# Clearing the semaphores straight behind the waiting drain, without the plain drain in between

## The chip, the cores and the metric

The kernel runs on one core of one Trainium2 chip. The metric is the device time of one execution in microseconds; the medians of several runs are compared. Besides the time there is the **span**, from the first to the last of the program's own instructions, which the profile of one run shows. Most numbers below with three decimals are the nanosecond stamps of the trace, read from the span's start; the views of the profile round them to one decimal, and narrow stretches of a view bracket them. A run counts as slow if it lies over 1.5% above the fastest of its kernel.

Three words recur. A **semaphore** is a counter by which transfers and engines signal that they are done. A **barrier** is a place where every engine reports and waits until all have. A **drain** is an instruction for an engine's sequencer, the part that reads its instructions; what it waits for is told in the prediction.

I call **closing** the time from the end of GpSimd's last wait for stores to the end of the span. It is what the change works on.

## The reference

Two arrays of 32 x 256 x 1024 floats are interleaved element by element:

```
result = zeros((batch, seq, dim * 2), float32)
result[..., 0::2] = x
result[..., 1::2] = y
```

No arithmetic is done. 67.11 MB are read and 67.12 MB written, among them 8 KB of zeros that the kernel stores first and overwrites.

## The kernel before

Inputs are loaded in tiles of 128 partitions x 8192 floats by SyncE's queue, VectorE copies x to the even and y to the odd columns of an output tile, and ScalarE's queue stores each tile of 128 x 8192 floats:

```python
    for lw in lwidths:
        # (cut: tiles and access patterns)
        nc.sync.dma_start(out=xtile, in_=xs)
        nc.sync.dma_start(out=ytile, in_=ys)
        # (cut: two halves of the width, each:)
            nc.vector.tensor_copy(out=otile[:, 0::2], in_=xsub)
            nc.vector.tensor_copy(out=otile[:, 1::2], in_=ysub)
            nc.scalar.dma_start(out=os_, in_=otile)
```

When the program is built, the framework adds a closing block. In it SyncE would wait for all transfers, an all-engine barrier would follow, and GpSimd would clear the semaphores. The kernel already edits that block: the wait is handed to GpSimd, and the first barrier is cut out.

```python
    last = nc.main_func.blocks[-1]
    tail = last.instructions
    waits = [i for i in tail
             if i.engine == mybir.EngineType.SP
             and not i.sync_info.on_update and i.sync_info.on_wait]
    clear = next(n for n, i in enumerate(tail) if i.opcode == "ISA")
    # (cut: assertions)
    last.instructions = [
        copy.replace(i, engine=mybir.EngineType.Pool) for i in waits
    ] + tail[clear - 1 :]
```

As built, GpSimd's part of the block is: four pure waits for transfer semaphores (two each), a drain that waits for VectorE's semaphore, a **plain drain** (`tail[clear - 1]`), the clear of semaphores 99 to 107, and then GpSimd's share of a barrier over all five engines, which has a drain of its own. The builder marks the plain drain as one that comes ahead of the reset of a range of semaphores; the other two lack the mark.

Of the kernel before, what the change touches and what calls it, by code (L numbers as in the profile page):

```python
# [3 lines left out]

# [4 lines left out]


@with_exitstack
def _interleave(
    ctx: ExitStack,
    tc: tile.TileContext,
    x: bass.AP,
    y: bass.AP,
    out: bass.AP,
):
    nc = tc.nc  # L20
    P = 128

    total = 1
    for s in x.shape:
        total *= s

    WL = 8192
    WS = 4096

    xf = x.rearrange("b s d -> (b s d)")  # L30
    yf = y.rearrange("b s d -> (b s d)")
    of = out.rearrange("b s d -> (b s d)")

    fp32 = mybir.dt.float32

    xpool = ctx.enter_context(tc.tile_pool(name="xp", bufs=2))
    ypool = ctx.enter_context(tc.tile_pool(name="yp", bufs=2))
    opool = ctx.enter_context(tc.tile_pool(name="op", bufs=2))

    lwidths = [WL] * (total // P // WL)  # L40
    assert sum(lwidths) == total // P


    wpool = ctx.enter_context(tc.tile_pool(name="wp", bufs=1))
    zero = wpool.tile([16, 128], fp32, name="zero")
    nc.vector.memset(zero, 0.0)  # L46
    first = dataclasses.replace(of, offset=0, ap=[[2 * WL, 16], [1, 128]])
    nc.scalar.dma_start(out=first, in_=zero)

    start = 0  # L50
    for lw in lwidths:
        xtile = xpool.tile([P, WL], fp32, name="xtile")[:, :lw]
        ytile = ypool.tile([P, WL], fp32, name="ytile")[:, :lw]

        xs = dataclasses.replace(xf, offset=start, ap=[[lw, P], [1, lw]])
        ys = dataclasses.replace(yf, offset=start, ap=[[lw, P], [1, lw]])
        nc.sync.dma_start(out=xtile, in_=xs)
        nc.sync.dma_start(out=ytile, in_=ys)

        soff = 0  # L60
        while soff < lw:
            width = min(WS, lw - soff)
            otile = opool.tile([P, 2 * WS], fp32, name="otile")[:, : 2 * width]
            os_ = dataclasses.replace(
                of,
                offset=2 * start + 2 * soff,
                ap=[[2 * lw, P], [1, 2 * width]],
            )
            xsub = xtile[:, soff : soff + width]
            ysub = ytile[:, soff : soff + width]  # L70
# [3 lines that stand above are left out]
            soff += width  # L74

        start += P * lw
    assert start == total


def kernel(tc, x, y, out):  # L80
    nc = tc.nc
    _interleave(tc, x, y, out)
    tc.close()
    tc.compile()  # L84


    blocks = nc.main_func.blocks
    opening = blocks[0].instructions
    at, moved = next(
        (b, i)  # L90
        for b in blocks[1:]
        for i in b.instructions
        if i.engine == mybir.EngineType.SP and i.opcode == "DMACopy"
    )
    assert not moved.sync_info.on_wait
    body = at.instructions
    body.remove(moved)
    gate = next(
        n
        for n, i in enumerate(opening)  # L100
        if i.engine == mybir.EngineType.SP and i.opcode == "Drain"
    )
    opening.insert(gate, moved)
    at.instructions = body
    blocks[0].instructions = opening




    last = nc.main_func.blocks[-1]  # L110
    tail = last.instructions
    waits = [
        i
        for i in tail
        if i.engine == mybir.EngineType.SP
        and not i.sync_info.on_update
        and i.sync_info.on_wait
    ]
    clear = next(n for n, i in enumerate(tail) if i.opcode == "ISA")
    assert tail[clear].engine == mybir.EngineType.Pool  # L120
    assert tail[: len(waits)] == waits
    last.instructions = [
        copy.replace(i, engine=mybir.EngineType.Pool) for i in waits
    ] + tail[clear - 1 :]


# [1 line left out]
_INS = ['x', 'y']  # L128
_OUTS = [((32, 256, 2048), 'float32')]


# [23 lines left out]
```

## Time and profile before

| | before |
|---|---|
| time, median of the first 3 runs | 316.22 us (315.30 to 316.36) |
| span of the profiled run | 314.7 us |
| end of the last wait for stores | 314.108 us |
| closing | 0.594 us |

The profile's lines on the transfers, the closing and the three GpSimd drains stand in the prediction, with the way to read them.

### The profile page before, as it was taken

Reading aid. Unit: us, or ns where it says so; the run is one execution under the profiler, and the core shown is the slowest. Engines: PE = TensorE matmul, PEld = TensorE weight load, DVE = VectorE, ACT = ScalarE, POOL = GpSimd, SP = SyncE. Lnnn points to the kernel's source line nnn. Section 1 sums busy time; section 2 is a strip of 40 time slices with the busy share of each in tenths; the row PEclk is TensorE's granted clock in tenths of the full one; section 3 lists DMA queues with packets and bytes.
Section 4 is the critical chain, followed back from the end, with each engine's and each line's share of the span. In section 5 each row is a group of like instructions: output and inputs, shape, how many; then the busy total and the mean of one; then the engine's idle time right before and its main releaser. Section 6 shows DMA issues by size and latency. Waiting matters only on the chain.

```text
span 314.7 us, 141 instructions
## 1 busy us (share of the span) xinstructions
DVE 72.8 (23%) x33; POOL 0.2 (0%) x4
## 2 busy tenths in 40 slices
DVE  0433002223022320223103241041500405014500
POOL 0000000000000000000000000000000000000000
DMA  9999999999999999999999999999999999999996
GB/s 355 441 425 379 450 416 450 416 450 412 454 412 454 412 462 404 462 404 462 404 462 404 462 404 458 408 458 408 458 408 458 408 458 408 458 408 458 408 458 279
DMA packets 4640, 134.23 MB, mean 427 GB/s; under 512 B 528, under 2 KB 544, under 8 KB 544
## 3 DMA queue, kind: packets, MB, share of 16 engines
q1 hardware_dynamic: 2304, 67.11, 49.9%
q10 hardware_dynamic: 2336, 67.12, 49.4%
HBM read 67.11 MB, written 67.12 MB: 427 GB/s over the span
## 4 chain that ended last, share of the span: by engine, by line
DMA 83%; DVE 11%; DVEq 1%; issue 0%
DMA out_dram<-otile 76%; DMA ytile<-in_y_dram 7%; DVE otile L72 6%; DVE otile L71 5%; DVEq L84 1%; DVEq L71 0%
## 5 line engine op out<-in xcount | busy, mean ns | idle before, releaser
L71 DVE COPY otile<-xtile 128x4096 f32<-128x4096 f32 x16 | 36.6, 2295 | 190.5 <-DMA out_dram<-otile 179.0
L72 DVE COPY otile<-ytile 128x4096 f32<-128x4096 f32 x16 | 36.6, 2292 | 35.2 <-DMA ytile<-in_y_dram 35.2
L46 DVE MEMSET zero<- 16x128 f32 x1 | 0.2, 165 | 0.9 <-PEq L139 0.9
L139 POOL MEMSET const-bfloat16-1.0<- 128x1 bf16 x1 | 0.1, 101 | 0.0
L139 POOL MEMSET const-uint8-127<- 128x1 uint8 x1 | 0.1, 101 | 0.0
L139 POOL MEMSET const-float32-0.0<- 128x1 f32 x1 | 0.1, 98 | 0.2 <-issue 0.2
L139 POOL MEMSET const-float32-1.0<- 128x1 f32 x1 | 0.1, 98 | 0.0
## 6 DMA issues: line engine op xcount, KB each, us to landing
out_dram<-otile ACTq DMA_DIRECT2D x16, 4096.0 KB, 29.7
xtile<-in_x_dram SPq DMA_DIRECT2D x8, 4096.0 KB, 43.1
ytile<-in_y_dram SPq DMA_DIRECT2D x8, 4096.0 KB, 60.2
out_dram<-zero ACTq DMA_DIRECT2D x1, 8.0 KB, 6.6
```

What stands on the lines that cost most here:

```text
L46: nc.vector.memset(zero, 0.0)
L71: nc.vector.tensor_copy(out=otile[:, 0::2], in_=xsub)
L72: nc.vector.tensor_copy(out=otile[:, 1::2], in_=ysub)
L84: tc.compile()
L139: nc = _bacc.Bacc("TRN2", target_bir_lowering=False, num_devices=1)
```

## The change

The plain drain is left out, so that the clear comes straight behind the waiting drain:

```diff
-    waits = [
-        i
-        for i in tail
-        if i.engine == mybir.EngineType.SP
-        and not i.sync_info.on_update
-        and i.sync_info.on_wait
-    ]
+    wait = tail[0]
     clear = next(n for n, i in enumerate(tail) if i.opcode == "ISA")
 ... (assertions cut)
     last.instructions = [
-        copy.replace(i, engine=mybir.EngineType.Pool) for i in waits
-    ] + tail[clear - 1 :]
+        copy.replace(wait, engine=mybir.EngineType.Pool)
+    ] + tail[clear:]
```

Its intent is to shorten the path behind the last store by one instruction that has nothing to wait for.

More of the change, by code (lines that the diff above doesn't have):

```diff
@@ L111 @@
     tail = last.instructions
-    waits = [
-        i
-        for i in tail
-        if i.engine == mybir.EngineType.SP
-        and not i.sync_info.on_update
-        and i.sync_info.on_wait
-    ]
+    wait = tail[0]
     clear = next(n for n, i in enumerate(tail) if i.opcode == "ISA")
+    assert wait.engine == mybir.EngineType.SP and wait.opcode == "Drain"
+    assert wait.sync_info.on_wait and not wait.sync_info.on_update
     assert tail[clear].engine == mybir.EngineType.Pool
-    assert tail[: len(waits)] == waits
     last.instructions = [
-        copy.replace(i, engine=mybir.EngineType.Pool) for i in waits
-    ] + tail[clear - 1 :]
+        copy.replace(wait, engine=mybir.EngineType.Pool)
+    ] + tail[clear:]
 _INS = ['x', 'y']
```

## The prediction

> **What bounds the kernel now.** I read the page first, then the source-line view of the line that the closing instructions carry, then that view again in stretches of some 10 to 100 ns, to see the order of the last half microsecond. Of the page, these lines carry it:
>
> ```profile
> span 314.7 us, 141 instructions
> DVE 72.8 (23%) x33; POOL 0.2 (0%) x4
> DMA  9999999999999999999999999999999999999996
> HBM read 67.11 MB, written 67.12 MB: 427 GB/s over the span
> DMA 83%; DVE 11%; DVEq 1%; issue 0%
> ```
>
> The third line gives the busy share of the 16 DMA engines, in tenths, for 40 slices: 39 slices are nearly full and only the last one falls off. 134.23 MB pass in 314.7 us. VectorE, which does all the arithmetic, is busy for 23%, and its copies lie beside transfers. So the time is one long transfer, framed by an opening of under 1 us and a closing of about 2 us. The chain line of the page is to be read with care: it follows the last engine work back, and the last engine work is a VectorE copy that ends near 299.3 us. What comes later, the last store and the closing, isn't in it at all. For that I take the windows view, whose columns are the stretch, its length, VectorE and GpSimd busy time, TensorE clock, DMA share and GB/s:
>
> ```profile
> 306.00:312.00 6.00, 0.00 (x0) 0.00 (x0) 1.00 1.01 437
> 312.00:313.75 1.75, 0.00 (x0) 0.00 (x0) 1.00 0.05 19
> 313.75:314.11 0.36, 0.00 (x0) 0.00 (x0) 1.00 0.00 0
> 314.11:314.70 0.59, 0.00 (x0) 0.00 (x0) 1.00 0.00 0
> ```
>
> The transfer runs at full rate up to about 312, then few packets are left. In the last two rows none starts. This is where the change lies. The source-line view of the closing names each kind of sequencer instruction there, with count, shortest, median and longest duration in ns, and the start of the first and last one in us:
>
> ```profile
> L84 POOLq EVENT_SEMAPHORE  x6: 17/43/9673, 282.0 to 314.6; - x6
> L84 POOLq DRAIN  x3: 34/41/70, 314.2 to 314.4; - x3
> L84 PEldq DRAIN  x1: 8/8/8, 0.9 to 0.9; - x1
> L84 SPq DRAIN  x1: 130/130/130, 228.9 to 228.9; - x1
> L84 DVEq DRAIN  x1: 4475/4475/4475, 294.9 to 294.9; - x1
> L84 ACTq DRAIN  x1: 152/152/152, 299.7 to 299.7; - x1
> L84 POOLq EVENT_SEMAPHORE_RANGE_CLEAR  x1: 92/92/92, 314.3 to 314.3; - x1
> ```
>
> The 9,673 ns instruction is the wait for the last two stores. It ends just before 314.11: the stretch from 314.11 to 314.15 holds nothing on this line. The drains of the other four engines began at 0.9, 228.9, 294.9 and 299.7 us, so all four have long reached the closing barrier and wait there for GpSimd. After 314.11 GpSimd's sequencer is thus the only one with anything to do, and whatever it does lies on the path that sets the end, one instruction after the other.
>
> Three narrow stretches of the same view separate the three GpSimd drains. From 314.15 to 314.20, from 314.21 to 314.30 and from 314.43 to 314.50 they show, in that order:
>
> ```profile
> L84 POOLq DRAIN  x1: 41/41/41, 314.2 to 314.2; - x1
> ...
> L84 POOLq DRAIN  x1: 70/70/70, 314.2 to 314.2; - x1
> ...
> L84 POOLq DRAIN  x1: 34/34/34, 314.4 to 314.4; - x1
> ```
>
> The first (41 ns) carries the wait for VectorE's semaphore, long satisfied. The second (70 ns) has neither wait nor update. Then follows the clear (92 ns), then the third drain (34 ns), which belongs to the closing barrier. Empty stretches at 314.20 to 314.21, 314.30 to 314.31 and 314.42 to 314.43 show that each is followed by a short gap before the next.
>
> **What the Trainium skill says.** "Perfetto Trace Analysis", section "Sequencer-only Instruction (DRAIN, etc)", says that the profile of such an instruction covers its execution alone; fetch and decode lie outside. The trace agrees: there are gaps between these instructions, in which none is shown. So the 70 ns isn't the whole price; a gap goes with it. "PSUM — Partial Sum Buffer" says, in the rule of its example of an unsafe increment, that a drain waits for its engine to become fully idle. The trace agrees: VectorE's drain lasted 4,475 ns behind two copies of some 2,290 ns each. GpSimd has only four memsets of about 100 ns, all in the first half microsecond, so nothing is left to wait for. "VectorE: DVE Perf Modes", section "The DRAIN you can't avoid", gives some 12 ns for a drain of the runtime's own code. The idle TensorE's 8 ns is of that size, GpSimd's 34 to 70 ns are not; I use the trace's own. And "Perfetto Trace Analysis", section "Roofline", gives about 435 GB/s as the sum of one core's 16 DMA engines. This trace has 427 over the span and 437 late in it. An estimate from that page, 134.23 MB over 435 GB/s, is 308.6 us: the bulk can hardly give.
>
> **The change part by part.**
> - *Removed:* one GpSimd drain, the second. The listing of the built programs shows the same number of working instructions on each engine; only drains and pure waits are left out of it, so I compared the closing block as built: 18 instructions before, 17 after, with exactly that drain missing. The edit reads as if it might also drop waits, because it picks one wait where the old text gathered all. But there is a single waiting drain at that point, and it is split later into four pure waits and the 41 ns drain. All of them are in the changed program as well.
> - *Added and moved:* nothing. Transfers, copies, semaphores and the barrier are the same.
> - *Its worth:* the empty stretches bound it. The first drain ends before 314.20 and the second starts before 314.22; the clear starts after 314.31. The removed drain's 70 ns plus one gap makes about 100 ns: for the gap I take about 27 to 29 ns, from the finer start times of the trace (second drain at 314.220, clear at 314.319: 99 ns from start to start). All of it lies on the path, since the other engines wait at the barrier. Nothing of it lies beside other work.
> - *Sum:* 316.22 us - 0.10 us = 316.12 us. The measured time is 1.8 us longer than the span (316.52 against 314.7 in the profiled run), for work outside the program's own instructions; the change doesn't touch it.
>
> 0.10 us is 0.03% of the time. The three runs before lie between 315.30 and 316.36 us, a spread of 1.06 us, ten times the gain.
>
> **The rivals.**
> 1. *The clear takes over the drain's time.* The middle drain is the longest of the three. If it spent its extra 30 ns on something that must settle anyway, such as the arrival of semaphore traffic, the clear or the drain behind it would become longer. For it: 70 against 41 and 34 ns. Against it: the engine has been idle since the first half microsecond, and the drain just before it took only 41. It would make the saving 0.07 us or less, down to nothing.
> 2. *The end is set by the transfers anyway.* If another engine were late at the barrier, the drain would be hidden. Against it: the latest other drain started at 299.7 us and took 152 ns, over 14 us before. It would leave 316.22 us.
> 3. *A late completion becomes visible.* Without the drain the clear runs 0.1 us closer to the last completion of the store, and a straggler could then disturb the next execution. Against it: the waits ask for the full count on all eight transfer semaphores, so no completion is left when the clear starts; and the check for races passes. It would show as a wrong result or a hang, not as a time.
> 4. *The bulk moves by chance.* The length of the transfer varies by about 1 us from run to run with nothing changed. This doesn't depend on the change, but the measured difference can have either sign from it. It gives the width of my range.
>
> **Range and chances.** The saving is between 0 and 0.13 us by rivals 1 and 2, so the centre is 316.1. The width comes from rival 4 alone: the spread of the runs before, some tenths wider on the upper side because the profiled run was at 316.52. I put 8 times in 10 at 315.3 to 316.7 us. 2% of the time is 6.3 us. The whole closing after the last wait is 0.59 us in the span, so removing all of it couldn't make 2%; nor can one drain fewer add 6 us. I leave 1% on each side for a disturbed run.
>
> **What would show it right or wrong.** In the changed profile GpSimd should have two drains in place of three on the closing line, near 41 and 34 ns, with 140 instructions in all. The distance from the end of the 9,673 ns wait to the span's end should fall from 0.59 to about 0.49 us. The clear should keep its 92 ns. A clear or first drain that is longer by 50 ns or more would speak for the first rival; an unchanged 0.59 us would refute the sum. The DMA rate and all that lies before 312 us should be as before, except for chance. The prediction is wrong as a whole if the time leaves the range with that distance at 0.49 us: then the bulk moved, and the drain isn't the cause.

## More of the kernel before

One more view is needed later. It is the chain of work that ended last, in order of time, of the kernel before; the columns are start, length and what the time went to.

```profile
0.78 21.44 DMA ytile<-in_y_dram
...
26.77 42.19 DMA out_dram<-otile
...
73.58 34.10 DMA out_dram<-otile
...
267.23 27.52 DMA out_dram<-otile
```

The second of these is the long piece: by its end the first two pairs of input loads and the first two stores have landed, all by way of the same 16 DMA engines. The chain reaches its next store at 73.58 us.

## The result and the profile after

The changed kernel took 315.55 us in the median of 6 runs (315.39 to 316.06), the kernel before 316.19 us in the median of 6 (315.30 to 316.36). The ratio is 0.9988, with a 95% interval of 0.9975 to 1.0002. Ratios here are the mean time of one kernel's fast runs over that of the other's of the same rounds, so they aren't quite the ratio of the medians. The results were correct, in this run and in all those below.

These are the page's lines of the changed kernel that answer to those of before:

```profile
span 313.6 us, 140 instructions
DVE 72.8 (23%) x33; POOL 0.2 (0%) x4
DMA  8999999999999999999999999999999999999997
HBM read 67.11 MB, written 67.12 MB: 428 GB/s over the span
```

One instruction fewer, the same work on VectorE, and DMA engines as full as before. The span is 1.1 us shorter, though, eleven times the 0.1 us that was expected of the drain. The source-line view of the closing shows what the drain had to do with it:

```profile
L84 POOLq EVENT_SEMAPHORE  x6: 17/43/9662, 280.3 to 313.5; - x6
L84 POOLq DRAIN  x2: 34/38/41, 313.1 to 313.3; - x2
L84 POOLq EVENT_SEMAPHORE_RANGE_CLEAR  x1: 92/92/92, 313.2 to 313.2; - x1
```

The 70 ns drain is gone, the other two kept 41 and 34 ns, and the clear kept 92 ns. By the stamps, the last wait ends at 313.073 us and the span at 313.570 us: the closing is 0.497 us, against 0.594 us. The drain was worth **0.097 us**.

The other 1.035 us lie before the end of the last wait (314.108 - 313.073), where nothing was changed. The chain of the changed kernel tells where:

```profile
0.78 21.14 DMA ytile<-in_y_dram
...
26.47 40.91 DMA out_dram<-otile
...
72.00 34.09 DMA out_dram<-otile
...
265.62 28.08 DMA out_dram<-otile
```

It is 0.30 us ahead at 26.47 us, and 1.58 us ahead at 72.00, because the long piece took 40.91 us in place of 42.19. The pieces of some 34.1 us that follow are alike, and the piece near the end gives back 0.56 us. So the lead arises in the first 72 us, during which the removed drain hasn't yet been reached in either kernel: GpSimd gets to it only after the last store.

### The profile page after: what moved, and what is told of

It reads as the page before. It is cut to its first block, busy times and chain, and to the rows that moved or that the text cites. A ratio compares the mean times of both kernels' runs of the same rounds, so it can differ in the third digit from the quotient of the medians.

```text
span 313.6 us, 140 instructions
## 1 busy us (share of the span) xinstructions
DVE 72.8 (23%) x33; POOL 0.2 (0%) x4
## 4 chain that ended last, share of the span: by engine, by line
DMA 83%; DVE 11%; DVEq 1%; issue 0%
DMA out_dram<-otile 76%; DMA ytile<-in_y_dram 7%; DVE otile L72 6%; DVE otile L71 5%; DVEq L84 1%; DVEq L71 0%
```

## The experiments

**The question.** The trace says 0.10 us for the drain and some 1 us for transfers that the edit doesn't touch; the times of several runs say 0.64 us between the medians. My theory: the drain is worth 0.10 us, and the rest is chance in the transfers. The rival: leaving the instruction out also changes the bulk, for instance through the program's length or layout. Ten submissions were run, four of them without an edit. Those of one group ran on the same chip and share the runs of the kernel before: the first four below are one group, the drain behind the clear and the kernel without a barrier belong to the group of the other order, and the drain without its mark and the forty idle drains are the third.

### The kernel before against itself

The file is the kernel before, with no edit.

> The kernel before, unchanged, against itself. Theory (one drain is worth 0.10 us, the other 0.5 us of the measured gain is chance in the transfers): ratio 1.000 within its interval, yet single runs between about 315.3 and 316.5 us. Rival (the change also moves the bulk by about 0.5 us): runs of this kernel stay near 316.2 us, hardly any near 315.4. The closing, from the end of the last GpSimd wait to the span's end, is 0.59 us in either case.

Measured: 315.77 us in the median of 5 runs (315.52 to 316.07), against 316.28 us of the 11 runs of the same kernel beside it (315.75 to 316.69). Ratio 0.9989, interval 0.9976 to 1.0002. The closing is 0.593 us.

**An unchanged kernel got the gain that the change had got** (0.9988). The first lines of its chain also look like those of the changed kernel, not like those of the first profile of its own code:

```profile
26.46 40.95 DMA out_dram<-otile
...
72.03 34.09 DMA out_dram<-otile
```

This doesn't leave the rival much: the fast opening comes without the edit. My theory expected 1.000 as the ratio, which lies within the interval, if near its end.

### The changed kernel again

No edit to the changed kernel.

> The changed kernel once more. Theory: 0.1 us under the runs of the kernel before on average, with an interval that holds both 0.9997 and 1.000; the closing is 0.50 us. Rival (the change moves the bulk): ratio near 0.998 again, 0.6 us under.

Measured: 315.67 us (5 runs, 315.60 to 316.10), ratio 0.9988, interval 0.9976 to 0.9999, closing 0.497 us. Alone, this ratio fits the rival, and its interval just leaves out the 1.000 that the theory wanted in it. Beside the unchanged kernel of the same group it doesn't: the medians differ by 0.10 us and the means by 0.02 us, in opposite directions (315.774 here, 315.752 there).

### Forty more drains on the path

```diff
     last.instructions = (
         [copy.replace(i, engine=mybir.EngineType.Pool) for i in waits]
+        + extra   # 40 copies of tail[clear - 1]
         + tail[clear - 1 :]
     )
```

> Forty more plain drains behind the removed one, before the clear. Theory (70 ns of execution and about 29 ns of gap each): +40 x 0.099 = +3.96 us, a time near 320.1 us, ratio 1.0125; all of it in the closing, which grows from 0.59 to about 4.55 us. Rival (a drain without anything to wait for costs nothing where the runtime's closing work runs after it): time unchanged within 0.5 us. Second rival (only the first of several drains takes 70 ns, the rest as little as the 34 ns one): 40 x about 0.063 = +2.5 us.

Measured: 319.14 us (4 runs, 319.01 to 320.05), ratio 1.010, interval 1.0085 to 1.0116. The median is 3.37 us above that of the unchanged kernel of the same group, and 2.86 us above that of the 11 runs beside it; the interval amounts to 2.7 to 3.7 us. By the trace the closing grew from 0.593 to 4.044 us, by 3.451 us, or 0.086 us for each drain:

```profile
L84 POOLq DRAIN  x43: 40/59/70, 313.4 to 317.1; - x43
```

The first two of the marked drains took 70 ns, the other 39 took 59 ns, with gaps of 26 or 27 ns between them. So 3.96 us was too much, because I had taken 70 ns for all of them, and the second rival's 2.5 us too little. The interval, too, holds neither. The first rival is refuted: nothing behind the program hides a drain. Profiled time less span is 1.83 us here and 1.82 us in the kernels before and after.

### The drain kept, but ahead of the waits

```diff
     last.instructions = (
+        [tail[clear - 1]]
-        [copy.replace(i, engine=mybir.EngineType.Pool) for i in waits]
+        + [copy.replace(i, engine=mybir.EngineType.Pool) for i in waits]
-        + tail[clear - 1 :]
+        + tail[clear:]
     )
```

> The drain is kept but moved ahead of the waits for the stores, where GpSimd idles anyway: 141 instructions as before. Theory (only its place on the closing path costs): the closing is 0.50 us as in the changed kernel and the time is the changed kernel's within 0.3 us. Rival (one instruction fewer in the program is what matters): the time is that of the kernel before, the closing 0.59 us.

Measured: 315.55 us (6 runs, 315.45 to 316.45), ratio 0.9988, closing 0.490 us. The program has as many instructions as before and yet the closing of the changed kernel. The place counts, not the number. The moved drain took 76 ns in its new place. The waiting drain took 34 ns in place of 41, which makes the closing 7 ns shorter than that of the changed kernel; why, I can't say.

### Both kernels once more, in the other order

> The changed kernel, submitted ahead of the kernel before this time. Theory (the drain is worth 0.10 us, and a resubmitted kernel comes out at a ratio near 0.999 whatever it holds, as the unchanged one did): ratio about 0.9985 to 0.9990, and 0.1 us under the next run, give or take 0.25 us. Rival (the change itself is worth 0.5 us and the unchanged kernel's 0.9989 was the accident): 0.5 us under the next run.

> The kernel before, unchanged, for the second time. Theory: again a ratio near 0.999, its interval reaching about 1.000, and 0.1 us above the run ahead of it, give or take 0.25 us. Rival: ratio 1.000, 0.5 us above. The closing is 0.59 us in both cases.

Measured on another chip: the changed kernel 315.39 us (6 runs, 315.27 to 316.38), ratio 0.9989; the unchanged one 315.65 us (6 runs, 315.48 to 316.74), ratio 0.9996, interval 0.9981 to 1.0011. Means: 315.613 and 315.832, a difference of 0.22 us, where the group before had given -0.02. Both fit 0.10 us and the stated width. It is the first pair that excludes 0.5 us: by an estimate from the scatter of the single runs, the standard error of its difference is 0.14 us, and that of this pair 0.26 us, too wide to do so alone. The closings are 0.497 and 0.593 us. The profile of this unchanged kernel has the slow opening again:

```profile
26.53 42.42 DMA out_dram<-otile
...
73.57 34.10 DMA out_dram<-otile
```

So the same code has its long piece at 42.19, 40.95 and 42.42 us in three profiles. The trace shows what goes with it. Of the 16 completions that each transfer gives, the last came 0.6 us after the last but one at the final store of the first profile of before (313.515 and 314.079 us), and 0.1 us after it in the changed kernel's (312.920 and 313.044 us): one part of the transfers lags in the slow profiles. (Slow here means the opening.)

All twelve profiles fall into these two kinds. In seven the long piece took 40.85 to 41.09 us, and the last completion of the final store came at most 0.13 us after the last but one; in five it took 42.19 to 43.27 us, and the last completion came 0.26 to 1.08 us after. What starts the lag isn't settled by these runs. The five slow profiles are all of kernels with at least three drains in the closing, which looks like the rival; but two profiles of such kernels were fast, and the spans of the single runs speak against it. With the closing taken off (that of the profile), their means are 313.31 us for the unchanged and 313.46 us for the changed kernel on the first chip, 313.44 and 313.29 us on this one: two differences of 0.15 us, of opposite sign.

### The drain behind the clear

```diff
     last.instructions = (
         [copy.replace(i, engine=mybir.EngineType.Pool) for i in waits]
-        + tail[clear - 1 :]
+        + [tail[clear], tail[clear - 1]]
+        + tail[clear + 1 :]
     )
```

> The drain is kept, but placed behind the clear, in front of the barrier's own drain. Theory (its price is execution plus gap anywhere on the closing path): closing 0.58 to 0.60 us as before, with the clear 0.10 us earlier. It also tells why the removed drain took 70 ns: if a drain straight behind a drain is the slow case, the two behind the clear take about 34 and 59 to 70 ns; if it was slow for another reason, its place behind the clear shows another time. Rival (a drain ahead of the clear serves the clear): clear longer than 92 ns.

Measured in a single look (state unknown, 316.08 us): closing 0.594 us, as before. The clear kept 92 ns, so nothing that the drain did for it had to be made up. In its new place the drain took 70 ns, and the barrier's own, now straight behind a drain, 34 ns as ever. Both parts of the guess about consecutive drains fell: the slowness belongs to this drain, not to its place behind another one.

### The drain without its mark

The drain is replaced by a copy of the barrier's own, which lacks the mark of a reset. In the built program the two differ in that mark and in name alone.

```diff
     last.instructions = (
         [copy.replace(i, engine=mybir.EngineType.Pool) for i in waits]
-        + tail[clear - 1 :]
+        + [copy.replace(plain, name="I-990")]   # plain: the barrier's drain, looked up above (cut)
+        + tail[clear:]
     )
```

> The removed drain is replaced by a copy of the barrier's own drain, which carries no mark that a range of semaphores is about to be reset. Theory A (the mark makes it 70 ns): 34 to 41 ns in this place, closing 0.56 us. Theory B (a drain in the place ahead of the clear, or any second drain, is slow): 59 to 70 ns, closing 0.59 us. The time tells nothing here, as 0.03 us is far below its spread.

Measured in a single look (state unknown, 316.50 us): the drain in question took 34 ns, and the closing was 0.558 us.

```profile
L84 POOLq DRAIN  x3: 34/34/41, 314.2 to 314.4; - x3
```

Theory A holds. Half of the 70 ns goes with the mark, though it still had nothing to wait for. Why most of the forty marked drains came down to 59 ns stays open; the next run has more on it.

### Forty more drains where GpSimd idles

```diff
     last.instructions = (
-        [copy.replace(i, engine=mybir.EngineType.Pool) for i in waits]
+        extra   # the same forty drains
+        + [copy.replace(i, engine=mybir.EngineType.Pool) for i in waits]
         + tail[clear - 1 :]
     )
```

> The same forty extra drains as in the run that cost 3.4 us, but ahead of the waits, where GpSimd idles from about 0.7 to 280 us; the drain under study stays in its place. Theory (only what stands behind the last wait is on the path): the closing is 0.59 us, and the time is that of the kernel before within 0.3 us. Rival (a program pays for each instruction wherever it stands, in loading or in work at its end): about 3.4 us more, ratio 1.010.

Measured: 315.80 us (6 runs, 315.34 to 316.59), against 316.24 us of the kernel before in 11 runs; ratio 0.9993, interval 0.9976 to 1.0009. By medians that is 0.44 us less, by the ratio 0.2 us, where the theory had allowed 0.3 us. The closing is 0.592 us. The forty drains run from 0.735 us to about 4.2 us, beside the first loads, and no cost is seen: the interval's upper end is 0.3 us, not the 3.4 us that they cost behind the waits. It also speaks against the rival of program length, since forty instructions more cost nothing that one fewer could save.

```profile
L84 POOLq DRAIN  x3: 40/40/59, 314.2 to 314.5; - x3
```

These are the three drains of the closing. The one under study took 59 ns here in place of 70, though 310 us had passed since the forty, and the barrier's own 40 ns in place of 34. So what a drain takes also goes with what stands ahead of it in the program; whether through having run or through layout isn't shown. The closing kept its length because these differences and a gap that was 5 ns longer nearly cancel.

### The changed kernel without its barrier

```diff
     last.instructions = [
-        copy.replace(wait, engine=mybir.EngineType.Pool)
-    ] + tail[clear:]
+        copy.replace(wait, engine=mybir.EngineType.Pool),
+        tail[clear],
+    ]
```

> The changed kernel without its closing barrier: GpSimd waits, clears, and the program ends; the other engines end when their own work is done. This is to see whether what follows the last store can be shortened further. Theory (every instruction behind the last wait is on the path): in the changed kernel the clear ends 0.21 us after the last wait and the span ends 0.50 us after it, so the closing is 0.21 us and the time falls by 0.29 us, to a ratio near 0.998 with the offset of a resubmitted kernel. Rival (the work outside the program waits for the engines anyway and takes the barrier's time over): the closing falls to 0.21 us, but the time stays within 0.1 us of the changed kernel's, so that the time less the span grows from 1.8 to about 2.1 us.

Measured: 315.37 us (5 runs, 315.11 to 315.47), ratio 0.9982, interval 0.9968 to 0.9995, in the group of the "other order". The closing is 0.207 us, as the theory said:

```profile
L84 POOLq EVENT_SEMAPHORE  x4: 43/43/9663, 280.3 to 303.4; - x4
L84 POOLq DRAIN  x1: 41/41/41, 313.1 to 313.1; - x1
L84 POOLq EVENT_SEMAPHORE_RANGE_CLEAR  x1: 92/92/92, 313.1 to 313.1; - x1
```

0.290 us came off the span. Profiled time less span rose from 1.82 to 1.88 us, so 0.06 us is given back outside the program and 0.23 us is left. Its mean time, 315.320 us, is 0.29 us under that of the changed kernel in its group (315.613), and 0.51 us under the unchanged one's (315.832); the medians differ by 0.02 and 0.28 us. By the trace it is the shortest of all versions. Its single runs overlap with those of the others, so its lead in time over the changed kernel isn't shown by the runs alone.

## Why the prediction was right

- **Where the change lies.** Right. The path behind the last wait is GpSimd's alone. Drains behind it cost (forty: 3.45 us), drains ahead of it showed no cost (forty: a closing of 0.592 us, and times that are no longer).
- **What the drain costs.** Right: some 100 ns predicted, 97 ns measured (70 of execution and the rest gap). The Trainium skill's statement that the profile covers a sequencer instruction's execution alone ("Perfetto Trace Analysis", section "Sequencer-only Instruction (DRAIN, etc)") carried the step from 70 to 97, and the gaps in all closings agree with it. One instruction that the prediction shows doesn't: the last wait, of 9,673 ns. It waits for two semaphores. It starts at 304.435 us, just after the last store but one has landed (304.412), and ends at 314.108, just after the last (314.079). So its profile holds the second of its two waits, and the prediction's "wait for the last two stores" is the wait for the last one. The sum doesn't rest on that.
- **The first rival, that the clear takes the time over.** Refuted: the clear is 92 ns in every run, and the closing fell in full. The remark in it that the middle drain spends 30 ns more than the others pointed at something else, the mark of the reset: 34 ns without it.
- **The second rival, a drain hidden by a late engine.** Refuted by the same 0.497 us.
- **The third, a straggling completion.** No run gave a wrong result or hung; more than that isn't shown.
- **The fourth, chance in the bulk.** It is what most of the measured 0.64 us between the medians is made of. The unchanged kernel against itself gave 0.9989 and 0.9996. The range of 315.3 to 316.7 us holds the measured 315.55, and not the sum but the chance placed it 0.55 us below the centre. The times alone would have shown neither that the 0.10 us is there nor that it isn't; the stamps of the closing show it.

One thing stays open. All six resubmissions of kernels whose closing is 0.49 to 0.59 us came out under 1 (0.9988 to 0.9996), the two of the unchanged kernel and the one with idle drains among them. With intervals of about 0.0013 to either side that can be chance, or an offset of some 0.1% of runs beside the reference runs. It doesn't need the drain's removal in either case.

## What to carry to other kernels

Behind the last wait for stores, each instruction of the only engine that still works is paid in full, the gap that follows it included (86 to 97 ns for a marked drain here), so that block can be counted instruction by instruction; ahead of the wait the same instructions showed no cost. If the gain that such a count gives lies below the spread of the times, take the verdict from the stretch itself in the trace, and run the unchanged kernel against itself before believing a measured gain that is larger than the count.

## What the Trainium skill lacked or had wrong

- "VectorE: DVE Perf Modes", section "The DRAIN you can't avoid": some 12 ns for a drain of the runtime's own code. A program's own drain on GpSimd, with nothing to wait for, took 34 to 41 ns, or 59 to 76 ns with the mark of a semaphore reset; no page has these.
- "Perfetto Trace Analysis", section "Sequencer-only Instruction (DRAIN, etc)": it names the unreported decode without its size. Between GpSimd's drains and the clear the unreported stages together showed as 26 to 34 ns of gap, so that the removed 70 ns drain was worth 97 ns, and one of forty in a row 86 ns. It also puts the wait for semaphores outside the profile, but the last wait here, for two semaphores, showed 9,673 ns.
- No page has the duration of the instruction that clears a range of semaphores: 92 ns for nine of them, in every profile.
- No page says what the framework's closing barrier costs on one core: 0.29 us of the span, and about 0.23 us of the profiled time.
